# A two-layer trunk on one Trainium2 core: low weight parts held behind the row-closing chain, and a reordered LayerNorm, pooling split and activation-table load in layer 0

## The chip, the cores and the metric

The kernel runs on one core of one Trainium2 chip. The metric is device time in microseconds (us) from start to end of one execution. Three runs of the kernel before gave 2075.46, 2076.23 and 2077.74 us; the median, 2076.23 us, is the time that the prediction is measured against.

## The reference

A 256 x 2048 fp32 activation passes through two layers. Every sub-layer is `x <- x + RMSNorm_post(f(RMSNorm_pre(x)))`, and each layer has a mixer and an MLP:

```python
h = rms_norm(x, mix_pre_g[l]);  x = x + rms_norm(mixer(h), mix_post_g[l])
h = rms_norm(x, ffn_pre_g[l]);  a = relu(h @ w1);  x = x + rms_norm((a*a) @ w2, ffn_post_g[l])
# layer 0 mixer: z = h @ w_in (2048 -> 3072); u = z[:, :1024], v, gate = the other two thirds
#   y_pool = (trailing means over 2/4/8/16 frames of u, minus u) @ pool_w (4 groups), * pool_scale
#   y_conv = silu(layer_norm(depthwise_conv31(v * sigmoid(gate)) + b));  out = [y_pool, y_conv] @ w_out
# layer 1 mixer: B, C, u = h @ w_in (2048 -> 6144);  out = (B * conv3(C * u)) @ w_out
```

The hidden size of the MLP is 8192. The weights are read from memory once, some 387 MB in all, and the arithmetic is fp32.

## The kernel before

**Tiles.** The 256 frames are two rows of 128 (`t` = 0 and 1). A weight is streamed in blocks of 256 input channels by 512 output channels (512 KB each, `specs`, line 114). `prep_to` (line 166) loads a block on SyncE's DMA queue into one of four `raw` buffers, copies it on ScalarE into a rounded high part `whi` (line 173) and subtracts on VectorE to get the low part `wlo` (line 178). There are nine buffers each of `whi` and `wlo`. A `raw` buffer comes free only when the low part has been made from it. While layer 0's mixer runs up to its first half of `w_out`, GpSimd makes the low parts in VectorE's place (`lo_eng`, lines 507 and 631). Activations are split into high and low in the same way, so each product is three matmuls of 128x128 by 512 columns: high by high, high by low, low by high (`mms`, lines 212 to 227). `ahead` (line 252) calls `prep_to` four blocks ahead for row 0 and eight for row 1.

**From one sub-layer to the next.** The last output columns of a row are evacuated from PSUM (`mix_evac`, line 587, or `last_evac`, line 654: square with accumulation on ScalarE, product with the gain on VectorE). `mix_close` (line 594) then makes the row's reciprocal root: line 600, the root on ScalarE (line 601), and lines 320 and 322 to 324 on VectorE, one 128x1 operation after the other. `close_row` (line 343) adds the result to the residual in four pieces (line 355). `norm_chunk` (line 293) transposes each piece on TensorE (line 276), and `split_cols` (line 257) writes the transposed high part `xh` (ScalarE, line 262) and low part `xl` (VectorE, line 265). With these the next sub-layer's first product can run. For row 0 of that product `mms_wide` (line 229) is used: first all 32 matmuls that need only `whi` (lines 240 and 241), then the 16 that need `wlo` (line 248).

**Order.** The program is traced in the order of the Python code, with work put off by `later` until so many `tick`s have passed (`mms` ticks after every two blocks). Then the framework's scheduler orders the instructions of each engine once, at build time: it simulates the program, and an engine takes the ready instruction of the highest priority. `urgent` (line 329) raises the priority by 150 instructions. On the chip each engine and each DMA queue then works strictly in that order.

**Layer 0's mixer.** The gates take a sigmoid (line 518). The convolution's 248 multiply-adds on VectorE (line 421) run in the background, several per tick. `pool_sum` (line 448) multiplies by a window matrix into a PSUM tile, scales it into an SBUF tile `pd` (line 463) and splits that into `ph` and `pl` (lines 271 and 272); `pool_mix` (line 478) multiplies by `pool_w` (line 492). `ln_stats` (line 543) and `ln_apply` (line 556) make the LayerNorm and the swish of one row each: mean, squares, variance, square root on ScalarE (line 564), five VectorE operations for the reciprocal root, then normalisation, a sigmoid on ScalarE (line 579) and the split into the output projection's operands. Square roots and sigmoids lie in different activation tables, so between them stands an ACT_TABLE_LOAD. The output projection (lines 604 to 651) runs the pooled half of its columns first; the LayerNorm must be ready for the second half, whose order is the list in line 635.

Of the kernel before, what the change touches and what calls it, by code (L numbers as in the profile page):

```python
# [16 lines left out]
P = 128  # L17
D = 2048
T = 256
# [14 lines left out]
def trunk_kernel(  # L34
# [26 lines left out]
    def t512(shape=(P, CB), dt=F32):  # L61
        return tp.tile(list(shape), dt, tag="t512", name=nm("t"))
# [93 lines left out]
        seg[f"so{cb}"] = add_seg(sc_w_out[0], 0, KT, cb * CB)  # L156
    add_ffn(1)

    pool_lo = set()
    for key in ("f1_0_0_0", "sC0", "f1_1_0_0"):  # L160
        pool_lo |= set()
    wt = {}
    nxt = [0]
    lo_eng = [lambda i: dve]
# [1 line left out]
    def prep_to(i):  # L166
        while nxt[0] <= min(i, len(specs) - 1):
            src, nj = specs[nxt[0]]
            raw = wp.tile([P, 2 * CB], F32, tag="raw", name=nm("raw"), bufs=4)
            nc.sync.dma_start(raw.rearrange("p (j n) -> p j n", j=nj), src)  # L170
            hi = wp.tile([P, 2 * CB], F32R, tag="whi", name=nm("whi"))
            lo = wp.tile([P, 2 * CB], F32R, tag="wlo", name=nm("wlo"))
            act.copy(hi, raw)  # L173
            i_, on_pool = nxt[0], nxt[0] in pool_lo

            def low(raw=raw, hi=hi, lo=lo, on_pool=on_pool, eng=lo_eng[0](i_)):
                for s in ((slice(0, CB), slice(CB, 2 * CB)) if on_pool else (slice(None),)):
                    (pool if on_pool else eng).tensor_tensor(  # L178
                        lo[:, s], raw[:, s], hi.bitcast(F32)[:, s], ALU.subtract)

            low()
            wt[i_] = (hi, lo)
            nxt[0] += 1

# [118 lines left out]
    def row_ssq(t):  # L303
# [6 lines left out]
        dve.tensor_scalar(v, sumsq(parts), 1.0 / D, EPS, ALU.mult, ALU.add)  # L310
        return v

    def rsqrt(v, y=None, root=None):
        s = small()
        if root:
            root(s)
        else:
            act.activation(s, v, AF.Sqrt)
        y = y or small()
        dve.reciprocal(y, s)  # L320
        h = small()
        dve.tensor_scalar(h, y, v, y, ALU.mult, ALU.mult)
        dve.tensor_scalar(h, h, -0.5, 1.5, ALU.mult, ALU.add)
        dve.tensor_scalar(y, y, h, None, ALU.mult)
        return y

    ms, rr, nparts = {}, {}, {}
# [71 lines left out]
    ]  # L399
    for t in range(NT):  # L400
        row_scale(t)
    for i, tr in enumerate(rest):
        later(1 + i, tr)

# [43 lines left out]
    def pool_sum(g):  # L448

        ic = t512((P, T))  # L450
        nc.sync.dma_start(ic, inv_cnt[g * T : (g + 1) * T].partition_broadcast(P))
        p = pst()
        for c in range(2):
            ct = 2 * g + c
            o = p[:, c * T : (c + 1) * T]
            n = 0
            for s in range(2):
                for m in (uh[s], ul[s]):
                    pe.matmul(o, m[:, ct * P : (ct + 1) * P], pwin[s][:, g * T : (g + 1) * T],
                              start=n == 0, stop=n == 3)  # L460
                    n += 1
        pd = t512((P, 2, T))
        dve.tensor_tensor(
            pd, p.rearrange("p (c n) -> p c n", c=2),
            ic.unsqueeze(1).to_broadcast([P, 2, T]), ALU.mult,
        )
        ph = tp.tile([P, 2, T], F32R, tag="ph", name=nm("ph"), bufs=2)
        pl = tp.tile([P, 2, T], F32R, tag="pl", name=nm("pl"), bufs=2)
        split_plain(pd, ph, pl)
        pd_[g] = (ph, pl)  # L470
# [72 lines left out]
    def ln_stats(t):  # L543
        xc = cs_[:, :, t * P : (t + 1) * P]
        mean = pst()[:, :P]
        for ct in range(8):
            pe.matmul(mean, ones, xc[:, ct, :], start=ct == 0, stop=ct == 7)
        dve.tensor_tensor(xc, xc, mean.unsqueeze(1).to_broadcast([P, 8, P]), ALU.subtract)
        sqs = []
        for h in range(2):  # L550
            sq = t512((P, 4, P))
            act.activation(sq, xc[:, 4 * h : 4 * h + 4, :], AF.Square)
            sqs.append(sq)
        later(1, lambda: ln_apply(t, xc, sqs))

    def ln_apply(t, xc, sqs):
        tsl = slice(t * P, (t + 1) * P)
        var = pst()[:, :P]
        for ct in range(8):
            pe.matmul(var, ones, sqs[ct // 4][:, ct % 4, :], start=ct == 0, stop=ct == 7)  # L560
        v = t512((P, P))
        dve.tensor_scalar(v, var, EPS, None, ALU.add)
        s = t512((P, P))
        act.activation(s, v, AF.Sqrt)
        y = t512((P, P))
        dve.reciprocal(y, s)
        dve.tensor_tensor(v, v, y, ALU.mult)
        dve.tensor_tensor(v, v, y, ALU.mult)
        dve.tensor_scalar(v, v, -0.5, 1.5, ALU.mult, ALU.add)
        dve.tensor_tensor(y, y, v, ALU.mult)  # L570
        dve.tensor_tensor(xc, xc, y.unsqueeze(1).to_broadcast([P, 8, P]), ALU.mult)
        for h in range(2):
            z = t512((P, 4, P))
            for i in range(4):
                ct = 4 * h + i
                dve.tensor_scalar(z[:, i, :], xc[:, ct, :], pcol("ln_g", ct), pcol("ln_b", ct),
                                  ALU.mult, ALU.add)
            sg = t512((P, 4, P))
            act.activation(sg, z, AF.Sigmoid)
            if t == NT - 1 and h == 1:  # L580
                warm = small()
                act.activation(warm, sg[:, 0, 0:1], AF.Sqrt)
            dve.tensor_tensor(z, z, sg, ALU.mult)
            hi, lo = yT[2 + h]
            split_plain(z, hi[:, :, tsl], lo[:, :, tsl])
# [5 lines left out]
        act.activation(junk, ps, AF.Square, accum_out=parts[t][:, i % 4 : i % 4 + 1])  # L591
        dve.tensor_tensor(ms[t][:, cb * CB : (cb + 1) * CB], ps, gp, ALU.mult)  # L592

    def mix_close(t, parts, nxt_gain, final=False):

        base = small()
        dve.tensor_scalar(base, sumsq(parts[t][:, :3]), 1.0 / D, EPS, ALU.mult, ALU.add)
        last = parts[t][:, 3:4]
        v = small()
        dve.tensor_scalar(v, last, 1.0 / D, base, ALU.mult, ALU.add)  # L600
        r = rsqrt(v, root=lambda s: act.activation(s, last, AF.Sqrt, bias=base, scale=1.0 / D))
        close_row(t, r, nxt_gain, final)

    pss = {}
# [13 lines left out]
    for cb in (2, 3):  # L618
        ids = seg[f"o{cb}a"]
        for t in range(NT):  # L620
            prep_to(ids[-1] + 4)
            pss[cb, t] = psg()
            if (cb, t) == (2, 0):
# [1 line left out]
                for h in range(2):  # L625
                    new_yT(2 + h)
                for i in range(NT):
                    later(1 + i, lambda i=i: ln_stats(i))
            mms(pss[cb, t], lhs_y(t), ids, 0, True, False)
    parts = {t: sp.tile([P, 4], F32, tag="pt", name=nm("parts"), bufs=4) for t in range(NT)}  # L630
    lo_eng[0] = lambda i: dve
    for t in range(NT):
        ms[t] = mp.tile([P, D], F32, tag="m", name=nm("m"))
    gps = {}
    for cb, t in ((2, 0), (2, 1), (3, 0), (3, 1), (0, 0), (1, 0), (0, 1), (1, 1)):
        ids = seg[f"o{cb}b"]
        if cb not in gps:
            gps[cb] = post_gain(mix_post_g, 0, cb)
# [4 lines left out]
        else:  # L643
            ps = psg()
            mms(ps, lhs_y(t), ids, 8, True, True)
            o = part[t][:, cb * CB : (cb + 1) * CB]
            dve.tensor_tensor(o, ps, o, ALU.add)
            ps = o
        urgent(mix_evac, t, cb, ps, gps[cb], parts)
        if cb == 1:  # L650
            urgent(mix_close, t, parts, ("ffn_pre", 0))


    def last_evac(t, cb, ps, gp, parts):
# [6 lines left out]
    def ffn(l, nxt_gain, final=False):  # L661
# [5 lines left out]
        for e in range(NE):  # L667
# [33 lines left out]
            for cb, t in order:  # L701
# [12 lines left out]
                    gps[cb] = post_gain(ffn_post_g, l, cb)  # L714
                urgent(last_evac, t, cb, ps, gps[cb], parts)
                if cb == NCB - 1:
                    urgent(mix_close, t, parts, nxt_gain, final)

    ffn(0, ("mix_pre", KT))

# [60 lines left out]
    for cb in range(NCB):  # L781
        ids = seg[f"so{cb}"]
        gp = post_gain(mix_post_g, 1, cb)
        for t in range(NT):
# [2 lines left out]
            mms(ps, lhs_y(t), ids, 0, True, True)  # L787
            urgent(mix_evac, t, cb, ps, gp, parts)
            if cb == NCB - 1:
                urgent(mix_close, t, parts, ("ffn_pre", KT))  # L790

    ffn(1, None, final=True)

# [41 lines left out]
```

## Time and profile before

| | |
|---|---|
| median of three runs | 2076.23 us (2075.46 to 2077.74) |
| the profiled execution's own time | 2074.67 us |
| its span, first to last instruction | 2072.9 us |
| TensorE busy | 2041.4 us (98%) |
| VectorE busy | 1174.0 us (57%) |
| ScalarE busy | 1008.3 us (49%) |
| GpSimd busy | 153.5 us (7%) |
| DMA, mean over the span | 188 GB/s |

The profiled execution is 1.6 us below the median. The profile's times are microseconds from the start of the span. Matmuls are pipelined and their ends are modelled, so TensorE's busy time says when it had work in it, not that it worked at its best speed. A wait is put down to the engine and the line that ended it.

### The profile page before, as it was taken

Reading aid. Unit: us, or ns where it says so; the run is one execution under the profiler, and the core shown is the slowest. Engines: PE = TensorE matmul, PEld = TensorE weight load, DVE = VectorE, ACT = ScalarE, POOL = GpSimd, SP = SyncE. Lnnn points to the kernel's source line nnn. Section 1 sums busy time; section 2 is a strip of 40 time slices with the busy share of each in tenths; the row PEclk is TensorE's granted clock in tenths of the full one; section 3 lists DMA queues with packets and bytes.
Section 4 is the critical chain, followed back from the end, with each engine's and each line's share of the span. In section 5 each row is a group of like instructions: output and inputs, shape, how many; then the busy total and the mean of one; then the engine's idle time right before and its main releaser. Section 6 shows DMA issues by size and latency. Waiting matters only on the chain.

```text
span 2072.9 us, 24556 instructions
## 1 busy us (share of the span) xinstructions
PE 2041.4 (98%) x9253; PEld 1687.7 (81%) x9253; DVE 1174.0 (57%) x1522; ACT 1008.3 (49%) x1296; POOL 153.5 (7%) x83
## 2 busy tenths in 40 slices
PE   8999999999999999999999999999999999999998
PEld 7888778888888888887888888888888888888886
DVE  3797764455455455547655645674555464554545
ACT  6454664444444354445544444464544444353443
POOL 5887000000000000000000000000000000000000
PEclk9999999999999999999999999999999999999999
DMA  7665546556565556556454665655555565565653
GB/s 261 198 208 180 176 148 219 175 180 210 171 203 181 184 194 198 186 170 213 161 197 165 201 197 177 202 189 193 183 193 193 170 212 187 171 208 189 201 172 114
DMA packets 203078, 390.30 MB, mean 188 GB/s; under 512 B 12368, under 2 KB 14512, under 8 KB 202960
## 3 DMA queue, kind: packets, MB, share of 16 engines
q1 hardware_dynamic: 202656, 388.55, 56.7%
q8 instruction: 72, 1.18, 0.2%
q14 instruction: 46, 0.38, 0.1%
q0 software_dynamic: 256, 0.18, 0.0%
q10 hardware_dynamic: 48, 0.02, 0.0%
HBM read 386.60 MB, written 2.10 MB: 188 GB/s over the span
## 4 chain that ended last, share of the span: by engine, by line
PE 85%; DVE 2%; DMA 1%; issue 1%; ACT 0%; DVEq 0%; ACTq 0%
PE pg L224 27%; PE pg L226 27%; PE pg L225 27%; PE pt L276 2%; DVE wlo L178 1%; DVE x L355 1%; PE pg L248 1%; PE pg L241 0%; DMA gp<-in_mix_post_g_dram 0%; PE pg L240 0%; DMA raw<-in_ab_w_out_dram 0%; ACT whi L173 0%; DVE xl L265 0%; DMA raw<-in_sc_w_in_dram 0%; DVE m L592 0%
## 5 line engine op out<-in xcount | busy, mean ns | idle before, releaser
L178 DVE TENSOR_TENSOR wlo<-raw,whi 128x1024 fp32r<-128x1024 f32 x660 | 807.5, 1227 | 580.4 <-ACT whi L173 547.9
L173 ACT CAST whi<-raw 128x1024 fp32r<-128x1024 f32 x722 | 760.2, 1054 | 575.2 <-PE pg L226 383.1
L226 PE MATMUL pg<-whi,xl 128*128 128x512 f32 x1520 | 596.0, 393 | 0.0
L224 PE MATMUL pg<-whi,xh 128*128 128x512 f32 x1520 | 590.9, 390 | 0.8 <-ACT t L518 0.7
L225 PE MATMUL pg<-wlo,xh 128*128 128x512 f32 x1520 | 591.3, 390 | 0.0
L225 PE MATMUL pg<-wlo,ah 128*128 128x512 f32 x1024 | 398.3, 389 | 0.0
L224 PE MATMUL pg<-whi,ah 128*128 128x512 f32 x1024 | 398.1, 389 | 0.0
L226 PE MATMUL pg<-whi,al 128*128 128x512 f32 x1024 | 397.6, 391 | 0.0
L225 PEld LDWEIGHTS pg<-wlo,xh 128*128 128x128 f32 x1520 | 285.4, 188 | 59.1
L224 PEld LDWEIGHTS pg<-whi,xh 128*128 128x128 f32 x1520 | 285.5, 188 | 58.5 <-ACT t L518 1.1
L226 PEld LDWEIGHTS pg<-whi,xl 128*128 128x128 f32 x1520 | 285.4, 188 | 56.9
L225 PEld LDWEIGHTS pg<-wlo,ah 128*128 128x128 f32 x1024 | 192.2, 188 | 40.1
L224 PEld LDWEIGHTS pg<-whi,ah 128*128 128x128 f32 x1024 | 192.3, 188 | 39.3
L226 PEld LDWEIGHTS pg<-whi,al 128*128 128x128 f32 x1024 | 192.3, 188 | 39.3
L178 POOL TENSOR_TENSOR wlo<-raw,whi 128x1024 fp32r<-128x1024 f32 x62 | 147.7, 2421 | 46.4 <-ACT whi L173 46.1
L680 ACT ACTIVATE t<-pg,rr 128x512 f32<-128x512 f32 x64 | 43.9, 686 | 194.0 <-PE pg L226 192.8
L711 DVE TENSOR_TENSOR m<-pg,m 128x512 f32<-128x512 f32 x96 | 65.9, 687 | 74.6 <-PE pg L226 74.6
L224 PE MATMUL pg<-whi,yh 128*128 128x512 f32 x256 | 100.2, 392 | 1.6 <-ACT yh L271 1.5
L225 PE MATMUL pg<-wlo,yh 128*128 128x512 f32 x256 | 99.7, 390 | 0.0
L226 PE MATMUL pg<-whi,yl 128*128 128x512 f32 x256 | 98.5, 390 | 0.2 <-DVE yl L272 0.2
L421 DVE SCALAR_TENSOR_TENSOR acc<-pp,par,acc 128x256 f32<-128x256 f32 x240 | 96.3, 480 | 0.1
L272 DVE TENSOR_TENSOR al<-pt,ah 128x512 fp32r<-128x512 f32 x64 | 44.0, 688 | 74.8 <-ACT ah L271 74.7
(130 smaller groups left out, 902.9 us busy)
## 6 DMA issues: line engine op xcount, KB each, us to landing
raw<-in_ffn_w_dram SPq DMA_DIRECT2D x512, 512.0 KB, 4.7
raw<-in_sc_w_in_dram SPq DMA_DIRECT2D x96, 512.0 KB, 4.9
raw<-in_ab_w_in_dram SPq DMA_DIRECT2D x48, 512.0 KB, 4.6
raw<-in_ab_w_out_dram SPq DMA_DIRECT2D x32, 512.0 KB, 3.9
raw<-in_sc_w_out_dram SPq DMA_DIRECT2D x32, 512.0 KB, 5.4
x<-in_x_dram SPq DMA_DIRECT2D x8, 256.0 KB, 7.2
gp<-in_mix_post_g_dram SPq DMA_DIRECT2D x8, 256.0 KB, 5.9
gp<-in_ffn_post_g_dram SPq DMA_DIRECT2D x8, 256.0 KB, 4.6
```

Source lines behind the costliest of these rows:

```text
L173: act.copy(hi, raw)
L178: (pool if on_pool else eng).tensor_tensor(lo[:, s], raw[:, s], hi.bitcast(F32)[:, s], ALU.subtract)
L224: pe.matmul(ps, lh, wh, start=start and k == 0, stop=False)
L225: pe.matmul(ps, lh, wl, start=False, stop=False)
L226: pe.matmul(ps, ll, wh, start=False, stop=stop and k == n - 1)
L248: pe.matmul(ps, lhs(k)[0], wt[c][1][:, j * CB : (j + 1) * CB], start=False, stop=k == n - 1)
L272: dve.tensor_tensor(lo, src, hi.bitcast(F32), ALU.subtract)
L276: pe.transpose(p[:, j * P : (j + 1) * P], src[:, j * P : (j + 1) * P], ident)
L355: dve.scalar_tensor_tensor(xs[t][:, cs], ms[t][:, cs], s, xs[t][:, cs], ALU.mult, ALU.add)
L421: dve.scalar_tensor_tensor(a, src, wcol, a, ALU.mult, ALU.add)
L680: act.activation(rl, ps, AF.Relu, scale=rr[t])
L711: dve.tensor_tensor(dst, ps, dst, ALU.add)
```

## The change

1. `hold` gives the first eight low parts of the next sub-layer, and the first of the segment behind it, an ordering edge: seven may be placed on VectorE only behind row 0's last root step (line 324), the other two only behind row 1's. The edge orders the queue alone; no semaphore is added. It is used at three places: layer 0's mixer to its MLP, layer 0's MLP to layer 1's mixer, and layer 1's mixer to its MLP.
2. A one-column sigmoid is issued right after the first `row_scale`s.
3. `pool_sum` scales in place in PSUM; the split reads PSUM.
4. LayerNorm: both rows' statistics are urgent and on one tick, `ln_root` is taken out of `ln_apply`, and both rows' roots are traced ahead of both rows' applications.
5. The second half of the output projection takes (column block, row) in the order (2,0), (3,0), (2,1), (3,1), ... where it took (2,0), (2,1), (3,0), (3,1); and the sum with the stored part is made in PSUM.

```diff
+    def after(inst, first):
+        tc.add_manual_dep(
+            inst.ins, first.ins.name,
+            mybir.DependencyInfo(mybir.DependencyClass.NoSync, mybir.DependencyReason.SCHED_ONLY),
+            reason="row chain first")
+    def hold(ids, first):
+        for i in ids:
+            if i in lows:
+                after(lows[i], first)
+            else:
+                guards[i] = first
...
-            low()
+            i_ = nxt[0]
+            low = lo_eng[0](i_).tensor_tensor(lo, raw, hi.bitcast(F32), ALU.subtract)
+            lows[i_] = low
+            if i_ in guards:
+                after(low, guards[i_])
...
-        dve.tensor_scalar(y, y, h, None, ALU.mult)
+        last_step[0] = dve.tensor_scalar(y, y, h, None, ALU.mult)
...
     for t in range(NT):
         row_scale(t)
+    act.activation(small(), rr[NT - 1], AF.Sigmoid)
...
-        pd = t512((P, 2, T))
-        dve.tensor_tensor(
-            pd, p.rearrange("p (c n) -> p c n", c=2),
-            ic.unsqueeze(1).to_broadcast([P, 2, T]), ALU.mult,
-        )
+        pd = p.rearrange("p (c n) -> p c n", c=2)
+        dve.tensor_tensor(pd, pd, ic.unsqueeze(1).to_broadcast([P, 2, T]), ALU.mult)
...
         r = rsqrt(v, root=lambda s: act.activation(s, last, AF.Sqrt, bias=base, scale=1.0 / D))
+        hold(nxt_ids[:7] if t == 0 else nxt_ids[7:], last_step[0])
         close_row(t, r, nxt_gain, final)
...
-                    later(1 + i, lambda i=i: ln_stats(i))
+                    later(1, lambda i=i: urgent(ln_stats, i))
+                    later(3 + i, lambda i=i: urgent(ln_root, i))
+                for i in range(NT):
+                    later(4, lambda i=i: urgent(ln_apply, i))
...
-    for cb, t in ((2, 0), (2, 1), (3, 0), (3, 1), (0, 0), (1, 0), (0, 1), (1, 1)):
+    for cb, t in ((2, 0), (3, 0), (2, 1), (3, 1), (0, 0), (1, 0), (0, 1), (1, 1)):
...
-            dve.tensor_tensor(o, ps, o, ALU.add)
-            ps = o
+            urgent(dve.tensor_tensor, ps, ps, o, ALU.add)
...
-            urgent(mix_close, t, parts, ("ffn_pre", 0))
+            urgent(mix_close, t, parts, ("ffn_pre", 0), False,
+                   seg["f1_0_0_0"] + seg["f1_0_0_1"][:1])
...
-                    urgent(mix_close, t, parts, nxt_gain, final)
+                    urgent(mix_close, t, parts, nxt_gain, final,
+                           () if final else seg["sC0"] + seg["su0"][:1])
...
-                urgent(mix_close, t, parts, ("ffn_pre", KT))
+                urgent(mix_close, t, parts, ("ffn_pre", KT), False,
+                       seg["f1_1_0_0"] + seg["f1_1_0_1"][:1])
```

## Rows read from the trace of the kernel before

**Rows 1.** The page's first part: busy time of each engine (share of the span, instructions).

```profile
PE 2041.4 (98%) x9253; PEld 1687.7 (81%) x9253; DVE 1174.0 (57%) x1522; ACT 1008.3 (49%) x1296; POOL 153.5 (7%) x83
```

**Rows 2.** TensorE's waits: for whom, us in total, times, longest us.

```profile
PE pg L241 <- DVE xl L265: 5.8, 4, 2.7
...
PE pg L240 <- ACT xh L262: 4.0, 2, 2.2
PE pt L492 <- DVE pl L272: 2.5, 1, 2.5
PE pg L224 <- ACT yh L271: 1.5, 1, 1.5
...
PE pg L224 <- ACT t L518: 0.7, 1, 0.7
```

**Rows 3.** Three sub-layer changes: window, length, TensorE busy (instructions), granted clock, DMA.

```profile
256.90:278.30 21.40, 16.42 (x74) 0.84 0.46 145
979.40:1000.80 21.40, 16.50 (x74) 0.84 0.44 140
1346.30:1361.50 15.20, 14.18 (x70) 1.00 0.67 223
```

**Rows 4.** Timeline of TensorE, first change: start, us, instruction, idle before.

```profile
261.01 0.80 PE L240 MATMUL pg<-whi,xh 128*128 128x512 f32 x1 [2.24 <-ACT xh L262]
263.76 0.79 PE L241 MATMUL pg<-whi,xl 128*128 128x512 f32 x1 [1.96 <-DVE xl L265]
```

**Rows 5.** Timeline of VectorE, first change: row 0's closing chain.

```profile
249.29 1.22 DVE L178 TENSOR_TENSOR wlo<-raw,whi 128x1024 fp32r<-128x1024 f32 x1
...
254.72 0.21 DVE L324 TENSOR_SCALAR sm<-sm,sm 128x1 f32<-128x1 f32 x1
...
256.65 2.73 DVE L355 SCALAR_TENSOR_TENSOR x<-m,sm,x 128x512 f32<-128x512 f32 x4
```

**Rows 6.** VectorE's busy time at the first and the second change: window, length, busy.

```profile
249.20:272.00 22.80, 22.66 (x51) 0.85 0.65 208
970.80:994.80 24.00, 23.11 (x51) 0.86 0.61 198
```

**Rows 7.** Timeline of VectorE, third change: a low part ahead, then the chain.

```profile
1329.34 1.22 DVE L178 TENSOR_TENSOR wlo<-raw,whi 128x1024 fp32r<-128x1024 f32 x1
...
1337.09 0.20 DVE L600 TENSOR_SCALAR sm<-parts,sm 128x1 f32<-128x1 f32 x1
...
1337.90 0.21 DVE L324 TENSOR_SCALAR sm<-sm,sm 128x1 f32<-128x1 f32 x1
```

**Rows 8.** The page's DMA issues: KB each, median us to landing.

```profile
raw<-in_ffn_w_dram SPq DMA_DIRECT2D x512, 512.0 KB, 4.7
```

**Rows 9.** Timeline of ScalarE, first change: a high part that waits for its load.

```profile
259.64 1.05 ACT L173 CAST whi<-raw 128x1024 fp32r<-128x1024 f32 x1 [1.09 <-DMA raw<-in_ffn_w_dram]
```

**Rows 10.** Line 272 by tile up to 300 us: ns min/median/max; then its third in the timeline.

```profile
L272 DVE TENSOR_TENSOR pl<-t,ph x4: 683/1161/2657, 137.4 to 165.8; 128x512 fp32r<-128x512 f32 x4
...
161.65 1.64 DVE L272 TENSOR_TENSOR pl<-t,ph 128x512 fp32r<-128x512 f32 x1
```

**Rows 11.** Groups of VectorE's instructions by form: count, busy us, mean ns, idle.

```profile
L272 DVE TENSOR_TENSOR al<-pt,ah 128x512 fp32r<-128x512 f32 x64 | 44.0, 688 | 74.8 <-ACT ah L271 74.7
```

**Rows 12.** Timeline of ScalarE, start of layer 0: a cast, later the first sigmoid.

```profile
31.09 1.05 ACT L173 CAST whi<-raw 128x1024 fp32r<-128x1024 f32 x1 [1.19 <-DMA raw<-in_ab_w_in_dram]
...
56.06 1.28 ACT L518 ACT_TABLE_LOAD   x1
57.35 0.69 ACT L518 ACTIVATE t<-pg,rr 128x512 f32<-128x512 f32 x1
```

**Rows 13.** Timeline of VectorE, LayerNorm of row 0: a low part ahead of the root.

```profile
198.11 3.29 DVE L178 TENSOR_TENSOR wlo<-raw,whi 128x1024 fp32r<-128x1024 f32 x1 [4.31 <-ACT whi L173]
201.32 0.28 DVE L562 TENSOR_SCALAR t<-pt 128x128 f32<-128x128 f32 x1
```

**Rows 14.** Timeline of GpSimd: the last three low parts that it makes.

```profile
193.24 7.08 POOL L178 TENSOR_TENSOR wlo<-raw,whi 128x1024 fp32r<-128x1024 f32 x3 [6.17 <-ACT whi L173]
```

More of the change, by code (lines that the diff above doesn't have):

```diff
@@ L157, in trunk_kernel @@
     add_ffn(1)
-    pool_lo = set()
-    for key in ("f1_0_0_0", "sC0", "f1_1_0_0"):
-        pool_lo |= set()
+    lows, guards = {}, {}
+    def after(inst, first):
[9 more added lines that the diff above has]
+                guards[i] = first
     wt = {}
@@ L173, in prep_to @@
             act.copy(hi, raw)
[L174 to L179, printed above, removed]
-            low()
+            i_ = nxt[0]
[3 more added lines that the diff above has]
+                after(low, guards[i_])
             wt[i_] = (hi, lo)
@@ L311, in row_ssq @@
         return v
+    last_step = [None]
     def rsqrt(v, y=None, root=None):
@@ L553, in ln_stats, with ln_root @@
             sqs.append(sq)
-        later(1, lambda: ln_apply(t, xc, sqs))
-    def ln_apply(t, xc, sqs):
-        tsl = slice(t * P, (t + 1) * P)
+        ln_sq[t] = sqs
+    ln_sq, ln_r = {}, {}
+    def ln_root(t):
         var = pst()[:, :P]
         for ct in range(8):
-            pe.matmul(var, ones, sqs[ct // 4][:, ct % 4, :], start=ct == 0, stop=ct == 7)
-        v = t512((P, P))
+            pe.matmul(var, ones, ln_sq[t][ct // 4][:, ct % 4, :], start=ct == 0, stop=ct == 7)
+        vsy = t512((P, 4, P))
+        v, s, y = vsy[:, 0, :], vsy[:, 1, :], vsy[:, 2, :]
         dve.tensor_scalar(v, var, EPS, None, ALU.add)
-        s = t512((P, P))
         act.activation(s, v, AF.Sqrt)
-        y = t512((P, P))
         dve.reciprocal(y, s)
@@ L570, in ln_apply @@
         dve.tensor_tensor(y, y, v, ALU.mult)
+        ln_r[t] = y
+    def ln_apply(t):
+        tsl = slice(t * P, (t + 1) * P)
+        xc, y = cs_[:, :, tsl], ln_r[t]
         dve.tensor_tensor(xc, xc, y.unsqueeze(1).to_broadcast([P, 8, P]), ALU.mult)
@@ L592, in mix_evac, with mix_close @@
         dve.tensor_tensor(ms[t][:, cb * CB : (cb + 1) * CB], ps, gp, ALU.mult)
-    def mix_close(t, parts, nxt_gain, final=False):
+    def mix_close(t, parts, nxt_gain, final=False, nxt_ids=()):
         base = small()
```

## The prediction

> **What bounds the kernel now.** I read the page's busy times first: TensorE has work in it for 98% of the span [rows 1]. No other engine comes near that, so a change that leaves the matmuls alone can win only what TensorE loses while it waits or runs at half clock. Next I read TensorE's waits [rows 2]. The reader should see two kinds. At the changes of sub-layer it waits for the transposed activations of the next one: 5.8 us for `xl`, 4.0 us for `xh`. In layer 0 it waits 2.5 us for the pooled low part, 1.5 us for the LayerNorm's output and 0.7 us for the first sigmoid. Third, I read the three sub-layer changes as windows, from the last matmul of the old sub-layer to the first of the new one's row 1 [rows 3]. The first two take 21.4 us each, with a granted clock of 0.84 on the mean. As the clock has two levels, 2.4 and 1.2 GHz, some 0.16 x 2 x 21.4 = 6.8 us of each ran at the lower. The engine had stood still for 2.24 us and again for 1.96 us before and in that stretch [rows 4]. The third change takes 15.2 us at full clock. It holds the same 48 matmuls, with eight transposes fewer and four matmuls of the old sub-layer more, which about cancel. So the first two lose some 6 us against the third. The third still stands idle for 1.0 us of its window.
>
> Why the third is short is seen on VectorE. At the first change, between line 600 and the end of line 324 (249.3 to 254.9), each 128x1 step of row 0's chain has a 1.22 us low part in front of it, four in all, and line 355 starts only at 256.65 [rows 5]. At the third change no `whi` was ready, and the same chain took 1337.09 to 1338.1, about 1.0 us [rows 7]. That is nearly the order that the change asks for: an experiment which the kernel before already holds.
>
> **Part 1, the hold at the first two changes.** It removes no work. It moves four low parts, 4 x 1.2 = 4.9 us, from inside row 0's chain to behind it, so line 324 ends near 250.3 and line 355 can run some 5 us earlier, under matmuls of the old sub-layer that still run. The ceiling is then VectorE itself: from 249.2 to 272.0 it was busy 22.66 of 22.80 us, at the second change 23.11 of 24.00 us [rows 6]. All of that work (eight low parts, both rows' residuals, row 0's `xl`) stands before row 1's first product. With some 1.3 us for row 1's first `xl` and the hand-over (an estimate: twice a piece of line 355, 2.73 / 4 us [rows 5]), row 1 can begin at 273.3 and 996.1, where it began at 278.3 and 1000.8 [rows 3]. So the gain is at most 5.0 and 4.7 us in this order, some 2 us more each if row 1's residual pieces or `rr` move behind. The lower bound of a harmless outcome is nothing. The order matters too. The held low parts also hold `raw` buffers: the fifth block's load starts only when the first low part is made, now behind line 324, at about 251.5. The load takes 4.7 us [rows 8], and SyncE's queue keeps every later load, the gain's too, behind it. ScalarE's queue then has `xh` behind a cast that waits for its load; that was so before [rows 9]. With a cast of 1.05 us [rows 9] the fifth `whi` comes near 257.3. `mms_wide` wants it after a quarter of its matmuls and some transposes, 3 to 4 us in, near 260: just covered. I take 4.2 and 3.9 us, near the ceiling because the third change shows the order working.
>
> **Part 1, third change.** One low part that ran at 1329.34, in VectorE's idle time, must now wait for the chain [rows 7]: 1.2 us moves into the busy stretch. Against that, two low parts leave row 1's chain there, and part of the 1.0 us could go. I take 0, with ends -1.5 and +1.
>
> **Part 2, the early sigmoid.** The table load took 1.28 us directly ahead of the sigmoid that TensorE waited for [rows 12]. Without it the PSUM tile is freed 1.3 us sooner, more than the 0.7 us wait [rows 2]. The load moves to about 30 us, where ScalarE waits 1.19 us for a load before its cast [rows 12] and blocks are prepared ahead. I take 0.7, with ends 0 and 0.8.
>
> **Part 3, the pooled split from PSUM.** The four `pl` have one shape, yet took from 0.68 to 2.66 us, the third of them 1.64 [rows 10]; GpSimd's low parts run through that stretch. The form that reads one operand from PSUM takes 0.688 us on the mean of 64 [rows 11], though mostly without GpSimd beside it. So the fourth `pl`, for which TensorE waits, gets 2.0 us shorter, and the third, which stands ahead of it in the queue, 0.95 us. Together this exceeds the 2.5 us that TensorE waited [rows 2]. The PSUM tile is held longer, until `pl` is done instead of until line 463, and the next product takes its slot; that product needs `pl` anyway. I take 2.4, with ends 0 and 2.6.
>
> **Parts 4 and 5, LayerNorm and order.** The prize is the wait for `yh`, 1.5 us, and 0.2 us for `yl` [rows 2]. With (3,0) ahead of (2,1), row 1's operands are wanted one product of 24 matmuls later, over 5 us (48 take under 14 [rows 3]), which removes the 1.5 us. Two of five table loads fall away, 2 x 1.28 us [rows 12] of ScalarE. Against it, row 1's root (six operations of 0.28 us and up [rows 13], some 2 us, an estimate) may come between row 0's root and its application, and row 0 had no slack. In its favour, a low part of 3.29 us stood ahead of row 0's root [rows 13] and urgent work may pass it. I take 1.2, with ends -2 and +1.9. The sum in PSUM replaces one pass by one pass of the same size: 0, under matmuls. The gain rows are wanted one step later and their buffers freed one step later: 0, since the old projection's next matmuls cover it, 1 us or so if they don't.
>
> Here a rule speaks against the change. The row shows a two-operand subtraction on VectorE taking 3.29 us instead of 1.22 while GpSimd made its last three low parts, 193.24 to 200.3 [rows 13, 14]. The Trainium skill, SBUF — State Buffer, section Who interferes with whom, says that a VectorE instruction with two SBUF inputs and a GpSimd instruction that reads SBUF exclude each other, and that whichever comes second waits for the whole of the other. By that rule part 3's gain is real, but a root brought forward into GpSimd's last stretch would be held there instead.
>
> **The sum.** 4.2 + 3.9 + 0 + 0.7 + 2.4 + 1.2 = 12.4 us. Against the profiled execution's 2074.67 us that gives 2062.3. The median stands 1.6 us higher, so the forecast for it is 2063.8.
>
> **The rivals.**
> 1. *The loads become the bound.* The hold keeps all four `raw` buffers full until about 251.5, low parts come behind line 355, and blocks five to eight arrive one load time later; TensorE then waits for `whi` or `wlo` in `mms_wide` where it waited for `xl`. For it: ScalarE's cast already waits for its load [rows 9]. Against: the third change has nearly the same order and idles 1.0 us. Half of the hold's gain goes: 8.3 us in all, 2067.9; if all of it goes, 2071.9.
> 2. *The hold does nothing.* The first four low parts are traced before the instruction that they are to follow; if the edge is dropped, or the scheduler had this order anyway, only layer 0's 4.3 us remain: 2071.9.
> 3. *Row 0's LayerNorm becomes the wait.* Row 1's root ahead of row 0's application, and its two-operand products beside GpSimd's last low parts (2.4 us each): the LayerNorm part turns from +1.2 to -2, 2067.0. It alone stays faster.
> 4. *Slower.* The same place as rival 1, but with low parts behind both rows' residuals. The fifth block's load starts near 260, and 4.7 us of load, 1.05 of cast and 1.22 of low part make it 267, with three more behind it at 1.2 us each; TensorE idles long enough to fall to the lower clock at all three changes. The third, now whole, pays the 6 us that the first two pay; they lose 2 us more each, and layer 0 gives 4.3 back: 6 + 4 - 4.3 = 5.7 slower, 2081.9. It decides from where the hold costs more than 4.3 us in all.
>
> **How the numbers follow.** Some 0.2%, 4.2 us, is what a measurement of this kernel can tell from no change. The forecast with rival 3 beside it gets 0.63, rival 1 gets 0.17 (0.13 faster, 0.04 within), rival 2 gets 0.11 (on the edge: 0.04 faster, 0.07 within), rival 4 gets 0.09. So faster 0.80, same 0.11, slower 0.09. The range takes in the ceilings of parts 1 to 5 (5.0 + 4.7 + 1 + 0.8 + 2.6 + 1.9 = 16.0, and some 2 us of movable work: 2058) and reaches up over rivals 1 and 2 to 2073; rival 4 and strays, 0.15, stay outside.
>
> **What would show it.** Right: no low part between line 600 and line 324 at the three changes; line 355 begins near 251; windows like those of [rows 3] near 17 us at clock 1.00; the four `pl` at 0.69 us; no table load right ahead of the first gate's sigmoid; TensorE's waits for `xl` and `xh` under 3 us in all. Wrong: waits for `whi` or `wlo` in `mms_wide`, a clock below 1.00 at the third change, a new wait for `yh` of row 0, or a sub-layer change as long as before though the chain is short.

## The result, and the profile after

The changed kernel takes 2084.71 us (median of four runs, 2084.44 to 2086.92), against 2076.43 us for the kernel before beside it; the ratio is 1.004, 95% interval 1.0028 to 1.0053. It is slower by 8.3 us, where 2063.8 was forecast and 2073 was the upper end of the range. Its profiled execution took 2084.74 us, 10.07 more than that of before (2074.67).

Busy times, waits of TensorE, and the three sub-layer changes as windows (cut as those of [rows 3]; in the third, row 1's products now begin among row 0's and four more transposes fall in, so its length and the lag in the table below differ a little):

```profile
PE 2045.3 (98%) x9253; PEld 1691.8 (81%) x9253; DVE 1171.1 (56%) x1522; ACT 1007.0 (48%) x1295; POOL 152.8 (7%) x83
```

```profile
PE pg L252 <- DVE xl L276: 12.8, 6, 3.5
...
PE pg L251 <- ACT xh L273: 3.7, 3, 1.5
PE pg L235 <- ACT yh L282: 2.9, 1, 2.9
PE pg L237 <- DVE yl L283: 2.3, 1, 2.3
```

```profile
259.16:283.36 24.20, 17.24 (x74) 13.44 (x73) 20.22 (x56) 16.85 (x51) 0.00 (x0) 0.86 0.49 156
984.46:1007.20 22.74, 16.11 (x74) 12.64 (x73) 19.82 (x55) 16.65 (x51) 0.10 (x1) 0.92 0.52 167
1352.70:1372.10 19.40, 16.50 (x73) 12.70 (x71) 16.19 (x46) 15.26 (x48) 0.00 (x0) 0.91 0.58 198
```

(Window, length, busy time of TensorE, weight load, VectorE, ScalarE, GpSimd, granted clock, DMA.) Against [rows 2], the waits for `pl` and for the first sigmoid are gone. The wait for `xl` has more than doubled, from 5.8 to 12.8 us, and the LayerNorm's output is now waited for 5.2 us. Against [rows 3], the changes are 2.8, 1.3 and 4.2 us longer, and the third, which ran at full clock, now has 0.91. VectorE, ScalarE and GpSimd are no busier than in [rows 1], so no work was added. (New lines for old: low part 178 is now 189, its cast 187; residual 355 is 368; `xl` 265 is 276; line 600 is 616, and line 324 is 337.)

To see where the time went I compare TensorE's progress: both kernels do the same 8640 products of 512 columns, and the **lag** is the start of the k-th in one trace minus its start in before's. It is worked out from all rows of two timelines. Each is one execution. Before's took 2074.67 us, while the medians of its runs lie between 2076.2 and 2077.3, so a lag read at the end comes out some 2 us too high (run 1 below: +3.0 by the lag, 0.1 by the medians; run 3: -2.0 and -4.8). Single stretches scatter too: in the four runs without the hold or added work (1, 3, 4, 8) the three changes add -0.2 to +0.2, +0.6 to +0.8 and 0.0 to +0.6 us.

| stretch | forecast, us | measured in the kernel after, us |
|---|---|---|
| early sigmoid | -0.7 | -0.5 |
| pooled split | -2.4 | -2.6 |
| LayerNorm and order | -1.2 | +5.3 |
| first change | -4.2 | +2.8 |
| second change | -3.9 | +1.3 |
| third change | 0 | +3.9 |
| sum | -12.4 | +10.2 |

(At the sigmoid itself the lag falls by 1.0 us; the trace had been 0.5 us behind before's ahead of it.)

**The changes.** VectorE at the first one:

```profile
250.47 0.20 DVE L616 TENSOR_SCALAR sm<-parts,sm 128x1 f32<-128x1 f32 x1
...
251.68 0.22 DVE L337 TENSOR_SCALAR sm<-sm,sm 128x1 f32<-128x1 f32 x1
251.81 3.49 DVE L189 TENSOR_TENSOR wlo<-raw,whi 128x1024 fp32r<-128x1024 f32 x3
255.22 2.73 DVE L368 SCALAR_TENSOR_TENSOR x<-m,sm,x 128x512 f32<-128x512 f32 x4
...
268.33 2.35 DVE L189 TENSOR_TENSOR wlo<-raw,whi 128x1024 fp32r<-128x1024 f32 x2
270.60 2.73 DVE L368 SCALAR_TENSOR_TENSOR x<-m,sm,x 128x512 f32<-128x512 f32 x4
273.25 2.15 DVE L276 SCALAR_TENSOR_TENSOR xl<-pt,par,xh 128x128 fp32r<-128x128 f32 x8
```

The hold did what it says: no low part stands in row 0's chain, which now takes 1.4 us where it took 5.8 (line 600 at 249.16; [rows 5]), and the residual starts 4.75 us after the chain's first step, where it took 7.5. But two held low parts then stand between row 1's chain and row 1's residual, and all of this stands ahead of row 0's third and fourth `xl`. These start 22.8 us after the chain's first step; in before the third started at 269.75, 20.6 us after it. TensorE shows the consequence (start, us, instruction, idle before):

```profile
261.54 0.49 PE L251 MATMUL pg<-whi,xh 128*128 128x512 f32 x1 [1.47 <-ACT xh L273]
264.00 0.79 PE L252 MATMUL pg<-whi,xl 128*128 128x512 f32 x1 [1.97 <-DVE xl L276]
...
273.65 0.80 PE L252 MATMUL pg<-whi,xl 128*128 128x512 f32 x1 [3.52 <-DVE xl L276]
274.24 0.63 PE L251 MATMUL pg<-whi,xh 128*128 128x512 f32 x1
274.67 0.63 PE L252 MATMUL pg<-whi,xl 128*128 128x512 f32 x1
```

The first product began only 1.7 us earlier relative to what stood before it, although row 0's residual starts 2.7 us sooner after the chain's first step. ScalarE's queue shows why:

```profile
256.73 1.06 ACT L187 CAST whi<-raw 128x1024 fp32r<-128x1024 f32 x1 [3.25 <-DMA raw<-in_ffn_w_dram]
258.87 1.05 ACT L187 CAST whi<-raw 128x1024 fp32r<-128x1024 f32 x1 [1.09 <-DMA raw<-in_ffn_w_dram]
260.17 1.04 ACT L187 CAST whi<-raw 128x1024 fp32r<-128x1024 f32 x1 [0.25 <-DMA raw<-in_ffn_w_dram]
261.12 2.17 ACT L273 ACTIVATE xh<-pt,par 128x128 fp32r<-128x128 f32 x8
```

`xh` stands behind three casts that wait for their loads, and TensorE's wait of 1.47 us is a wait for these (1.43 us in much the same way at the second change). In before `xh` stood behind such casts as well, and TensorE waited 2.24 and 1.76 us. So the loads do not make the changes longer than before's, but TensorE, which had transposed the first pieces by 260.1, could not use them until 261.5.

Then TensorE stood 3.52 us for the third `xl` (before: 0.25), and its clock fell a second time (matmuls 0.43 us apart, later 0.23; granted clock 0.52 from 273.5 to 277). VectorE's dense stretch, from the chain's first step to the end of row 0's last `xl`, as in [rows 6]:

```profile
250.47:275.40 24.93, 24.19 (x51) 0.90 0.67 211
975.89:1000.81 24.92, 24.18 (x51) 0.93 0.66 211
1343.77:1366.60 22.83, 22.23 (x48) 0.93 0.66 219
```

It got longer, 24.9 us for 22.8: it has nine low parts where it had eight, as the first of the held seven had been made at 240.84, in idle time. At the third change 18.0 became 22.8, with one low part more (nine for eight), and with row 1's residual ahead of row 0's last `xl`, where before's came behind it. Before, then after:

```profile
1353.95 1.13 DVE L265 SCALAR_TENSOR_TENSOR xl<-pt,par,xh 128x128 fp32r<-128x128 f32 x4
...
1356.26 2.74 DVE L355 SCALAR_TENSOR_TENSOR x<-m,sm,x 128x512 f32<-128x512 f32 x4
```

```profile
1359.45 2.35 DVE L189 TENSOR_TENSOR wlo<-raw,whi 128x1024 fp32r<-128x1024 f32 x2
1361.71 1.12 DVE L276 SCALAR_TENSOR_TENSOR xl<-pt,par,xh 128x128 fp32r<-128x128 f32 x4
1362.75 2.73 DVE L368 SCALAR_TENSOR_TENSOR x<-m,sm,x 128x512 f32<-128x512 f32 x4
1365.40 1.12 DVE L276 SCALAR_TENSOR_TENSOR xl<-pt,par,xh 128x128 fp32r<-128x128 f32 x4
```

**The LayerNorm** on VectorE, then ScalarE, then what TensorE waited:

```profile
197.96 0.28 DVE L575 TENSOR_SCALAR t<-pt 128x128 f32<-128x128 f32 x1
...
199.48 0.23 DVE L575 TENSOR_SCALAR t<-pt 128x128 f32<-128x128 f32 x1
...
205.01 1.22 DVE L587 TENSOR_TENSOR cs__426<-cs__426,t 128x1024 f32<-128x1024 f32 x1
...
207.53 0.68 DVE L599 TENSOR_TENSOR t<-t,t 128x512 f32<-128x512 f32 x1
...
213.17 0.68 DVE L283 TENSOR_TENSOR yl<-t,yh 128x512 fp32r<-128x512 f32 x1
```

```profile
204.59 1.28 ACT L595 ACT_TABLE_LOAD   x1
...
209.78 0.61 ACT L282 CAST yh<-t 128x512 fp32r<-128x512 f32 x1
```

```profile
210.44 0.50 PE L235 MATMUL pg<-whi,yh 128*128 128x512 f32 x1 [2.92 <-ACT yh L282]
213.90 0.79 PE L237 MATMUL pg<-whi,yl 128*128 128x512 f32 x1 [2.26 <-DVE yl L283]
```

Row 1's root (from 199.48) and its application (205.01) run among row 0's steps, low parts come between them too, and row 0's `yl` is made at 213.17, 15.2 us after the root's first step (10.0 in before, 201.32 to 211.33). The clock was 0.76 from 211 to 225 (1.00 from 205 to 225 in before). By the lag TensorE loses 7.3 us at row 0's operands; 1.9 of it come back at row 1's, for which it no longer waits.

**The pooled split** came out as worked out; of the four `pl` (ns, min/median/max; [rows 10] had 683/1161/2657):

```profile
L283 DVE TENSOR_TENSOR pl<-pt,ph x4: 681/689/694, 135.8 to 162.8; 128x512 fp32r<-128x512 f32 x4
```

### The profile page after: what moved, and what is told of

The parts are those of the page before. It is cut to its first block, busy times and chain, and to the rows that moved or that the text cites. A ratio compares the mean times of both kernels' runs of the same rounds, so it can differ in the third digit from the quotient of the medians.

```text
span 2082.9 us, 24551 instructions
## 1 busy us (share of the span) xinstructions
PE 2045.3 (98%) x9253; PEld 1691.8 (81%) x9253; DVE 1171.1 (56%) x1522; ACT 1007.0 (48%) x1295; POOL 152.8 (7%) x83
## 4 chain that ended last, share of the span: by engine, by line
PE 94%; DVE 3%; DMA 1%; issue 1%; ACT 1%; DVEq 0%; ACTq 0%
PE pg L237 30%; PE pg L236 30%; PE pg L235 30%; PE pt L287 2%; DVE wlo L189 1%; DVE x L368 1%; DMA raw<-in_ab_w_in_dram 1%; PE pg L259 1%; PE pg L252 0%; PE pg L251 0%; ACT whi L187 0%; PE pt L503 0%; DMA raw<-in_ffn_w_dram 0%; DVE xl L276 0%; PE pt L473 0%
```

## The experiments

Four theories for the loss at the changes. A: VectorE's dense stretch sets their length, and the hold moves work into it. B: the hold is not the cause; something else in the change is (the delay that layer 0 hands on, or the clock). C: the held low parts keep the `raw` buffers, and loads come late. D, a finer form of A: the harm is in what is held behind row 1's chain. For layer 0 the question is which part of the new LayerNorm and order costs. Lags are against before's trace; medians carry the ratio to the runs of before beside them. The diffs are cut to the lines that matter: runs 1, 8 and 10 are edits of the changed kernel, 2, 3, 5 and 7 of the kernel before, 6 of run 2, and 4, 9 and 11 of run 3.

**1. The change without the hold.**

```diff
-        hold(nxt_ids[:7] if t == 0 else nxt_ids[7:], last_step[0])
```

> The changed kernel without the hold (the ordering edges); parts 2 to 5 stay. By the profiles of the two kernels, TensorE's matmuls stand 3.1 us earlier than before behind the pooled split, 2.3 us later behind the LayerNorm, and 5.1, 6.4 and 10.3 us later behind the three sub-layer changes. Theory A (each loss belongs to its own part: the LayerNorm part costs 5.3 us where it stands, the hold 8.0 us at the three changes): 2.3 us slower than before, about 2078.7 us, with the three changes as long as before. Theory B (the changes of sub-layer lose because layer 0 hands them over at another moment, not through the hold): they stay longer than before, 2082 us or more.

2077.38 us, ratio 1.0 (0.999 to 1.001): level with before, where A expected 2.3 us slower. The lag goes from -2.4 to +2.7 over the LayerNorm, and the three changes then add -0.2, +0.6 and 0.0. So the changes lose only with the hold, and layer 0's 5.1 us loss stands by itself. B falls.

**2. The kernel before with the hold alone.**

```diff
         r = rsqrt(v, root=lambda s: act.activation(s, last, AF.Sqrt, bias=base, scale=1.0 / D))
+        hold(nxt_ids[:7] if t == 0 else nxt_ids[7:], last_step[0])
```

> The kernel before with the hold alone (part 1). Theory A: no change in layer 0, then 2.8, 1.3 and 3.9 us lost at the three changes: 8.0 us slower, about 2084.4 us. Theory B: no loss at the second and third change, 2076 us or, as the prediction had it, 2068 us.

2081.29 us, ratio 1.0018 (1.0009 to 1.0028). The changes add 2.9, 0.5 and 2.1 us. By the medians the hold alone costs 4.0 us, half of the 8.0 that A expected; its ten executions spread from 2077.97 to 2083.97. With parts 2 to 5 beside it (the changed kernel against run 1) it costs 7.3. Why it costs less alone is open. (Another 2.4 us of lag is there before the first change; 1.5 of it came at the pooled split, whose code is that of before; run 7 shows the same 1.6 us there.)

**3. Early sigmoid and pooled split alone.**

```diff
+    act.activation(small(), rr[NT - 1], AF.Sigmoid)
...
+        pd = p.rearrange("p (c n) -> p c n", c=2)
+        dve.tensor_tensor(pd, pd, ic.unsqueeze(1).to_broadcast([P, 2, T]), ALU.mult)
```

> The kernel before with the early sigmoid and the pooled split from PSUM alone (parts 2 and 3). Theory A: 0.5 and 2.6 us earlier behind the first gate and the pooled mix, and the same from there on: 3.1 us faster, about 2073.3 us. Rival: TensorE arrives 3 us earlier at the LayerNorm's output, which does not come earlier, so the wait for it grows from 1.5 us by up to 3 us and the gain is given back: 2076 us.

2072.54 us, ratio 0.9977 (0.9967 to 0.9988). The lag is -2.9 behind the split and -2.0 at the end; by the medians it is 4.8 us. These two parts are faster than the kernel before, as forecast.

**4. The same with the new order list.**

```diff
-    for cb, t in ((2, 0), (2, 1), (3, 0), (3, 1), (0, 0), (1, 0), (0, 1), (1, 1)):
+    for cb, t in ((2, 0), (3, 0), (2, 1), (3, 1), (0, 0), (1, 0), (0, 1), (1, 1)):
```

> As the run with parts 2 and 3 alone, and the output projection's second half in the new order of column blocks and rows; LayerNorm and the sum as before. By the prediction's step the wait for row 1's LayerNorm, 1.5 us, goes: 4.6 us faster than before, about 2071.8 us. Rival: the new order wants the second block's low parts 5 us earlier, the scheduler puts them on VectorE ahead of row 0's LayerNorm, and row 0 becomes the wait: 2074 us or more.

2074.78 us, ratio 0.9988 (0.9979 to 0.9998). The lag of -3.4 becomes -1.3 at row 1's first LayerNorm operand: the list costs 2.1 us. Run 4, then run 3, at that place:

```profile
222.50 0.50 PE L235 MATMUL pg<-whi,yh 128*128 128x512 f32 x1 [2.06 <-ACT yh L282]
...
223.61 0.63 PE L236 MATMUL pg<-wlo,yh 128*128 128x512 f32 x1
224.03 0.63 PE L237 MATMUL pg<-whi,yl 128*128 128x512 f32 x1
```

```profile
222.49 0.50 PE L235 MATMUL pg<-whi,yh 128*128 128x512 f32 x1 [1.50 <-ACT yh L282]
...
223.29 0.39 PE L236 MATMUL pg<-wlo,yh 128*128 128x512 f32 x1
223.52 0.40 PE L237 MATMUL pg<-whi,yl 128*128 128x512 f32 x1
```

The wait for row 1 did not go; it grew from 1.50 to 2.06, since the evacuation of (3,0) on ScalarE, 0.58 us, now stands ahead of `yh`. Behind the longer wait the clock fell to half; behind the shorter it did not. The queue explains why there was nothing to win: in before, 54 products stand between row 0's first LayerNorm operand (210.64) and row 1's (225.34), room for the 24 of (2,0) and the 24 of (3,0) both, and in runs 3 and 4 the same 54 come, line by line in the same order. The list is the order of tracing, not that of TensorE.

**5. Before with VectorE 1.36 us fuller.** Two 0.68 us operations whose result is not used, behind row 0's residual at each change.

```diff
+        if t == 0 and not final:
+            for q in range(2):
+                d = t512()
+                dve.scalar_tensor_tensor(d, ms[t][:, q * CB : (q + 1) * CB], r, ms[t][:, (q + 2) * CB : (q + 3) * CB], ALU.mult, ALU.add)
```

> The kernel before with two more VectorE operations of 0.68 us (a product of row 0's columns with the root, whose result nobody reads) right behind row 0's residual pieces at each of the three changes: 1.3 us of work on VectorE, no buffer held, no load delayed. Theory A (from row 0's chain to row 0's last xl VectorE is dense, and each microsecond of work put into that stretch lengthens the change by as much): TensorE's matmuls fall 1.3 us or a little more behind at the first and at the second change, up to 1.3 at the third: some 3.5 us in all. Theory C (the hold costs through the loads that wait for the held raw buffers, not through VectorE's time): under 1 us in all.

2079.44 us (one run; before 2076.65). The changes add 1.6, 1.7 and 1.6 us. What is put into VectorE's stretch comes out of TensorE's time in full, with a little on top, as A says. At that rate the first low part, moved into the stretch out of idle time, costs its 1.2 us or a little more at each change; this is worked out, not measured by itself.

**6. The hold alone with five `raw` buffers** (and one `ph` and `pl` for two, to make room).

```diff
-name=nm("raw"), bufs=4)
+name=nm("raw"), bufs=5)
```

> The kernel with the hold alone, with five raw buffers in place of four (the space is taken from the pooled split, which has one buffer each for its halves in place of two). The hold alone lost 2.9, 0.5 and 2.2 us at the three changes. Theory C (held raw buffers delay the loads, and casts that wait for them stand ahead of xh on ScalarE): the loss at the changes falls from 5.5 us to under 2. Theory A (VectorE's stretch is dense): it stays within 1.5 us of 5.5.

2082.3 us (one run). The changes add 1.3, -0.1 and 6.4 us, 7.6 in all, outside both expectations. With a buffer more the loss is no smaller in the sum, so C is not its main cause. But the first two changes lose 1.2 us where run 2 lost 3.4, and the third 6.4 where it lost 2.1: a share of the loads at the first two is not excluded, and the `xh` rows above show them in the way there.

**7. The hold for row 0 only.**

```diff
-        hold(nxt_ids[:7] if t == 0 else nxt_ids[7:], last_step[0])
+        if t == 0:
+            hold(nxt_ids[:7], last_step[0])
```

> The kernel with the hold for row 0 alone: the eighth low part and the one behind it are free. Theory D (the part behind row 1's chain is what hurts: it puts two low parts and row 1's residual ahead of row 0's last xl): the loss of 5.5 us at the changes falls to 2 or less, and the waits of 2 us and more for the third piece of xl go. Theory A or C alone: it stays near 5.5 us, since the same work is in the stretch and the same buffers are held behind row 0's chain.

2075.16 us (one run). The changes add -0.6, -1.1 and +1.4 us. VectorE at the first:

```profile
266.18 2.35 DVE L189 TENSOR_TENSOR wlo<-raw,whi 128x1024 fp32r<-128x1024 f32 x2
...
268.83 1.13 DVE L276 SCALAR_TENSOR_TENSOR xl<-pt,par,xh 128x128 fp32r<-128x128 f32 x4 [0.24 <-ACT xh L273]
```

The two low parts fill time ahead of row 1's chain; row 0's third `xl` comes ahead of row 1's residual, 18.7 us after row 0's chain began (250.11) instead of 22.8. The condition for D is met, in one run: row 1's hold is the larger harm. That the first low part of row 0's hold eats most of what the rest gains is left to run 9.

**8. Sigmoid, split, and the new LayerNorm code, urgent but row by row**, with the old order list and the old sum, and no hold.

```diff
                 for i in range(NT):
                     later(1, lambda i=i: urgent(ln_stats, i))
                     later(3 + i, lambda i=i: urgent(ln_root, i))
-                for i in range(NT):
-                    later(4, lambda i=i: urgent(ln_apply, i))
+                    later(3 + i, lambda i=i: urgent(ln_apply, i))
```

> Parts 2 and 3 and the changed LayerNorm code, all of it urgent, but traced row by row (row 0's root, row 0's application, then row 1's), in the old list order and with the old sum; no hold. With both roots first the LayerNorm lost 5.3 us. If the loss comes from row 1's root and normalisation standing between row 0's steps, it goes here: 3 us faster than before at the end of layer 0's mixer, 2073 us or so. If it comes from the urgency (low parts and casts pushed aside and then in the way), it stays: 2 us slower than before.

2072.74 us (one run). The lag is -2.9 ahead of the LayerNorm and -3.2 behind it: no loss. Urgency and the split functions cost nothing. What is gone with the 5 us is both roots first, with row 1's work among row 0's, but also the new list and the sum in PSUM; run 10 keeps these two.

**9. A version made from the findings.** Sigmoid and split; row 1's Sqrt table load moved behind the split that TensorE waits for; the hold for row 0 alone, at the first two changes, without the first low part.

```diff
+        if t == 0 and nxt_ids and nxt_ids[0] != seg["f1_1_0_0"][0]:
+            hold(nxt_ids[1:7], last_step[0])
...
-                warm = small()
-                act.activation(warm, sg[:, 0, 0:1], AF.Sqrt)
...
             split_plain(z, hi[:, :, tsl], lo[:, :, tsl])
+            if t == NT - 1 and h == 1:
+                act.activation(small(), hi[:, 0, tsl][:, 0:1].bitcast(F32), AF.Sqrt, scale=0.0)
```

> The split from PSUM and the early sigmoid (2072.5 us together), the Sqrt table load of row 1's LayerNorm moved behind the split that TensorE waits for, and the hold kept for row 0 alone, without its first low part, at the first two changes. If VectorE's dense stretch sets the changes: the table load gives 1.2 to 1.3 us (the wait for row 1's yh falls from 1.5 to about 0.2), the hold gives 0.6 and 1.0 as in the run with row 0 held plus up to 1.2 each, because the first low part stays in idle time ahead of the chain: 2068 to 2070 us. If the hold is harmful in every form: about 2071.3 from the table load alone, or over 2073.

2066.13 us (five runs, 2066.05 to 2066.94), ratio 0.9952 (0.9938 to 0.9965): 10.5 us faster than before and below what was expected. On ScalarE the load now stands behind `yh`, which gives 1.2 us (lag -2.9 to -4.1):

```profile
220.63 1.22 ACT L282 CAST yh<-t 128x512 fp32r<-128x512 f32 x2 [0.24 <-DVE t L591]
221.87 1.28 ACT L595 ACT_TABLE_LOAD   x1
```

The changes add -2.7, -1.8 and +0.1 us. VectorE at the first:

```profile
244.60 0.20 DVE L610 TENSOR_SCALAR sm<-parts,sm 128x1 f32<-128x1 f32 x1
...
245.54 2.35 DVE L189 TENSOR_TENSOR wlo<-raw,whi 128x1024 fp32r<-128x1024 f32 x2
247.81 2.73 DVE L368 SCALAR_TENSOR_TENSOR x<-m,sm,x 128x512 f32<-128x512 f32 x4
...
261.99 1.11 DVE L276 SCALAR_TENSOR_TENSOR xl<-pt,par,xh 128x128 fp32r<-128x128 f32 x4
```

The residual starts 3.2 us after the chain's first step, and row 0's third `xl` 17.4 us after it. This last number goes with the change's length: 22.8 (after, +2.8), 20.6 (before, 0), 18.7 (run 7, -0.6), 17.4 (run 9, -2.7). Over all twelve kernels beside before it holds at the first change in sign: 17.4 to 18.7 goes with -0.6 to -2.7 (three kernels), 20.6 to 21.2 with -0.2 to +0.2 (four), 22.7 to 23.5 with +1.3 to +2.9 (five). It does not give the size (run 6: 23.4 and only +1.3), and it fails at run 2's second change, 18.5 and yet +0.5, where the fourth `xl` came only at 25.3. One more thing differs in run 9: TensorE waits 0.20 us for the first `xh`, where the changed kernel waited 1.47, for only two casts that wait for loads stand ahead of it. The early first low part, which frees its `raw` buffer, may pay through this as well; no run separates the two.

**10. The whole change with two repairs:** LayerNorm row by row as in run 8, hold for row 0 only as in run 7.

> The whole change with two things taken back: the LayerNorm goes row by row (still urgent, still with the new list of products and the sum in PSUM), and row 1's chain holds nothing. If these two places are the cause of the loss: layer 0 stands at -3 after the sigmoid and the split and at -1 to -3 after the LayerNorm (the new list cost 2.1 us there before), the first two changes give about 0 and the third costs up to 1.5; 2073 to 2075 us, not above the kernel before. If something else in the change costs: 2078 us or more.

2072.96 us, ratio 0.9984 (0.9975 to 0.9993). The lag stays at -3.3 up to row 1's operands, where the list costs 2.2 us as in run 4, so the order of the roots, taken back alone, saves 3 of the 5 us; the changes add -1.2, +0.2 and +3.2. Two places, taken back, turn 8 us slower into 4 us faster. The third change costs more here than the 1.4 us of run 7; why is open. (The execution with the trace, 2075.51 us, is the slowest of eleven, 2.6 above their median, and the lags are read from it.)

**11. Two of the low parts at each change on GpSimd,** no hold, table load as in run 9.

```diff
+    to_pool = {i for key in ("f1_0_0_0", "sC0", "f1_1_0_0") for i in seg[key][5:7]}
...
-            low = lo_eng[0](i_).tensor_tensor(lo, raw, hi.bitcast(F32), ALU.subtract)
+            low = (pool if i_ in to_pool else lo_eng[0](i_)).tensor_tensor(lo, raw, hi.bitcast(F32), ALU.subtract)
```

> No hold. The sixth and seventh low part of the next sub-layer's first eight are made on GpSimd at each change, and the Sqrt table load moved as in the combined kernel. If VectorE's amount of work sets the length of the changes: 2 x 1.2 us leave it at each, and the three changes shorten by 1 to 2.4 us each at the first two: 2067 to 2070 us. If GpSimd's reads hold VectorE's two-operand instructions up (as beside the pooled split: 1.64 and 2.66 us for 0.68): each GpSimd low part of 2.4 us costs as much as it saves, 2071 to 2074 us, with low parts and residual pieces on VectorE above 1.22 and 0.68 us.

2074.66 us, ratio 0.9993 (0.9984 to 1.0002): 8.5 us above run 9, and just above the worse of the two expectations. The changes add 1.7, 1.3 and 0.6. VectorE, then GpSimd:

```profile
251.44 6.61 DVE L369 SCALAR_TENSOR_TENSOR x<-m,sm,x 128x512 f32<-128x512 f32 x4
```

```profile
250.79 5.38 POOL L190 TENSOR_TENSOR wlo<-raw,whi 128x1024 fp32r<-128x1024 f32 x2 [53.14 <-ACT whi L188]
```

Row 0's residual took 6.61 us instead of 2.73: 3.9 us lost for 2.4 saved. The Trainium skill, SBUF — State Buffer, section Who interferes with whom, has such a VectorE instruction and a GpSimd read exclude each other; the row agrees.

## Why the prediction was wrong, point by point

**What held.** The view that TensorE sets the time and that the losses sit in its waits; the early sigmoid (0.7 forecast, 0.5 measured); the pooled split (2.4 and 2.6, all four `pl` at 0.69 us); that the hold is a real edge (rival 2 falls); that TensorE does not come to wait for `whi` or `wlo` in `mms_wide` (rival 1 as it stands falls: no such wait is in the list). Three of the prediction's own signs of being wrong came: a clock below 1.00 at the third change (0.91), a wait for `yh` of row 0 (2.92 us), and changes as long as before though the chain is short.

**The hold at the first two changes, 4.2 and 3.9 us.** The step that failed is "The ceiling is then VectorE itself", with 5.0 and 4.7 us worked out as if row 1 could begin when VectorE's work was done. In before VectorE was already dense up to 271.97 and row 1 began only 6.3 us later, since the 32 matmuls of `mms_wide` wait for row 0's `xl` piece by piece and then 16 more follow. What TensorE waits for is not the end of the stretch but the place of the third `xl` in it. Putting the chain first shortened nothing ahead of that place: the same low parts still stand there, nine now for eight. Two terms were left out. "It moves four low parts" should have been five of the seven, one of which had run in idle time at 240.84: 1.2 us (run 5 shows that such work costs its full length). And the two parts held behind row 1's chain got no term at all; they put row 1's work solidly ahead of row 0's third `xl` (run 7 against run 2: 3.5, 1.6 and 0.7 us). Of the first change's 2.8 us, 2.0 are longer waits (idle in the windows 6.96 us for 4.98) and 0.8 longer busy time, with the second fall of the clock. That some 6.8 us ran at half clock was read rightly, but the stall ahead of it was moved, not removed. A smaller term stood at nothing: "ScalarE's queue then has `xh` behind a cast that waits for its load; that was so before". It still cost TensorE 1.47 and 1.43 us at the first two changes, so the part of the gain that was to come through an earlier `xh` came only in part.

**The third change, 0 with an end at -1.5.** The low part moved into the dense stretch was seen, and its 1.2 us fit run 7's +1.4 there. "Two low parts leave row 1's chain" was taken for a gain; they left it for the place between chain and residual, and row 0's last `xl` moved behind both. That the third change "shows the order working" was the wrong inference: it has eight low parts in its stretch like the first two, and the stretch is short, 18.0 us, above all because row 1's residual stands behind row 0's last `xl` and not ahead of the third. The prediction had this place as an aside, "some 2 us more each if row 1's residual pieces or `rr` move behind", and put no term to it.

**LayerNorm and order, +1.2 with an end at -2.** Rival 3 named the mechanism, row 1's root ahead of row 0's application, and the row shows it; its price was 7.3 us at row 0's operands, 5.3 after what row 1's gave back, not 2. The bound counted the root alone; row 1's normalisation, low parts and casts came along, and waits of 2.92 and 2.26 us were followed by a clock of 0.76. The gain that was set against it, "row 1's operands are wanted one product of 24 matmuls later", read the list as TensorE's queue; the queue was in that order already, and the list by itself cost 2.1 us (run 4). The rule about GpSimd was not the cause: GpSimd's last low part ended at 196.95, row 1's root began at 199.48, and its reciprocal took 0.95 us like row 0's.

**Rival 4** had the sign and nearly the size (2081.9), with the price put at all three changes, but by another mechanism: late loads behind both rows' residuals, with TensorE waiting for low parts, a wait that the list does not have. Its chance of 0.09 was too low because the hold's harm was sought only in loads.

**Still open:** how the second change's loss comes to be half of the first's (of its 1.3 us, 0.6 to 0.8 are in the runs without the hold as well), why the hold costs 4.0 us alone and 7.3 with the other parts, what share the loads have at the first two changes, and the 3.2 us of the third change in run 10.

## What to carry to other kernels

Where an engine is dense between two waits, putting its critical chain first is worth only what it moves ahead of the next operand that is waited for: list the queue up to that operand in both orders, count the work ahead of it, and look for work that leaves idle time to join it. An edge for row 0 says nothing of row 1: hold as little as the chain needs, and leave what has a place in idle time there. The order in which a program is written is not that of the engine; read the built queue before pricing a swap.

## What the runs showed of the hardware

A wait of 1.50 us left TensorE's clock at full and one of 2.06 us at the same place was followed by half clock (runs 3 and 4: granted clock 1.00 and 0.57 from 222.4 to 226.4), which made 0.56 us more of waiting cost 2.1 us. Two low parts on GpSimd stretched four residual pieces from 2.73 to 6.61 us, more than the low parts would have cost on VectorE (2 x 1.2 us).
